# A decoder block's mixer with chunk matrices kept as 32x32 diagonal blocks, alternating small products, split attention scores and a solver tied to its place in VectorE's queue

## The chip, the cores and the metric

The kernel runs on one core of a Trainium2 chip. The metric is the time of one execution in device microseconds, from the first to the last instruction with what lies around them; lower is better. The five engines of the core are called PE (TensorE, matrix products), DVE (VectorE), ACT (ScalarE), POOL (GpSimd) and SP (SyncE, which issues most of the DMAs here). Each works through its own instructions in the order in which they are queued.

## The reference, cut to what matters

One decoder layer for 512 tokens of width 1024, in fp32. A projection of the normalized input feeds two mixers side by side, whose outputs are concatenated and projected back; an expert retrieval layer (PEER) and a gated embedding follow. The two mixers are what the change is about.

```python
def block(bi):                      # differential attention, 4 heads of 2 x 64, blocks of 128 queries
    s = jnp.einsum('bhcqd,bhckd->bhcqk', qb, k).astype(f32)
    causal = key_pos[None, :] <= (start + jnp.arange(Q_BLOCK))[:, None]
    pr = jax.nn.softmax(jnp.where(causal, s, -jnp.inf), axis=-1)
    a = pr[:, :, 0] - lam * pr[:, :, 1]
    return jnp.einsum('bhqk,bhkv->bhqv', a.astype(v.dtype), v)
...
def step(state, inp):               # RWKV-7, 8 heads of 64, one token after the other
    r_t, d_t, k_t, v_t, kk_t, a_t = inp
    sa = jnp.einsum('bhij,bhj->bhi', state, -kk_t)
    state = (state * d_t[:, :, None, :] + sa[..., None] * (kk_t * a_t)[:, :, None, :]
             + v_t[..., None] * k_t[:, :, None, :])
    return state, jnp.einsum('bhij,bhj->bhi', state, r_t)
```

## The kernel before

**Tiling.** The 512 tokens are four blocks b0 to b3 of 128, and a block is four chunks of 32 tokens for the RWKV mixer. Inside a chunk the recurrence is written as matrix products: for each head a matrix of products between the tokens is needed, of which only the pairs inside one chunk count. A block's matrix of a head has 128x128 entries, so the four 32x32 blocks on its diagonal are the ones that count; the rest is set to zero by a mask.

**Stages.** The mixer stage lies between about 125 and 440 us of the span; after it come the output projection, the expert layer and the tail, none of which the change touches, and each of which needs the whole of the mixer's output. The mixer has two phases.

- First phase, to about 277 us: `rw_prepare` runs for each block, woven with the projections of the attention's q, k and v (`acc` matmuls, whose operands are split into two fp32r parts, hi and lo). It makes four transposes (`ptr`), then the four masked matrices: `psA` products of beT and ktT with art, masked by DVE into `aab`, `arb`, `aak`, `ark` (L549 to L554), and two products of a masked matrix with v (`pg`, L569). `da_prepare` transposes q and k of the attention (`ptq`), and ACT copies them out.
- Second phase, from 277 us: per block `rw_solved` (`pwu`, `pmt`, `prp`), `rw_states` (four steps of `pst`), `rw_out` (`py`) and, per attention head, `da_block`: scores `psS` (L765, fp32, then L766, which adds the causal mask as a product with the identity), a row maximum on DVE (`sm`, L769), an exponential on ACT (L770), the weighted difference of two exponentials on DVE (`pexp`, L775), transposes (`pta`), the product with v (`po`). `ple_proj` (`accr` matmuls) is woven in.

**The solver.** `rw_solve(half)` inverts the chunk matrices of two blocks with 31 steps on DVE, each a product `sol_p` (L593) and a sum `sol_x` (L595). Half 0 runs in the first phase, half 1 in the second; its result goes to DRAM and comes back as `tt`, which `pwu` of block b2 needs first.

**What sets the order.** The code says in which order the pieces are emitted (generators that are woven), but a list scheduler then orders the instructions of each engine, which are executed in that order. `self.behind(x, y)` puts x after y in this order and nothing else. Tiles come from pools with a fixed number of buffers (tags `p2`, `p4`); a piece waits when its pool has none free.

## Time and profile before

| | us |
|---|---|
| median of 3 runs | 1839.75 (1837.05 to 1845.11) |
| the profiled execution | 1837.09 |
| its span, first to last instruction | 1835.4 |
| PE busy | 1728.9 (94% of the span) |
| DVE busy | 1425.6 (78%) |
| ACT busy | 746.7 (41%) |
| POOL busy | 604.7 (33%) |

The share of busy time is an average over all stages: PE's 94% comes mostly from the expert layer, after 600 us. A row of a group of instructions gives the line of the kernel, the engine, the operation, the tiles (output <- inputs), the shapes and the count; then the busy time, the mean of one in ns, and the idle time of the engine ahead of these instructions with what ended it. PE's matmuls overlap, so sums over them can exceed the time that passed; where that matters, starts are compared. An fp32 matmul is two PE instructions, an fp32r matmul one.

### The profile page before, as it was taken

What the parts mean: (1) busy time and instruction counts of PE and PEld (TensorE: products, weight loads), DVE (VectorE), ACT (ScalarE), POOL (GpSimd) and SP (SyncE); (2) the same over time, 40 slices, a digit from 0 to 9 for tenths busy, and PEclk for the clock granted to TensorE, in tenths of its full rate; (3) what the DMA queues carried; (4) which work ended last, traced back from release to release, by engine and by line L of the source; (5) the groups of instructions that cost most, each with busy time, mean ns of one, the idle gap of its engine ahead of it and who ended that gap; (6) DMA issues with size and microseconds to landing.
All of it is one profiled execution on the core that took longest, in us unless ns stands there. A gap on an engine that the chain in (4) does not pass through costs nothing.

```text
span 1835.4 us, 28662 instructions
## 1 busy us (share of the span) xinstructions
PE 1728.9 (94%) x10458; PEld 1468.2 (80%) x10458; DVE 1425.6 (78%) x3216; ACT 746.7 (41%) x1382; POOL 604.7 (33%) x425
## 2 busy tenths in 40 slices
PE   7889996998899888999999999999999999999998
PEld 6766764766777787998777888889899999999986
DVE  5366787675569998888888888887888888888885
ACT  5353332432345654444344333333333333333354
POOL 2650011111046663001111133234545555555530
PEclk9896996999999999999999999999999999999999
DMA  7451233433332343446666587778989898989891
GB/s 232 137 149 55 75 114 79 129 80 127 117 120 71 125 127 115 132 139 216 206 209 197 187 272 249 254 246 292 313 302 317 300 316 303 312 303 316 303 332 58
DMA packets 150417, 363.71 MB, mean 198 GB/s; under 512 B 43922, under 2 KB 58510, under 8 KB 150148
## 3 DMA queue, kind: packets, MB, share of 16 engines
q1 hardware_dynamic: 113412, 227.65, 38.7%
q0 software_dynamic: 36864, 134.23, 21.5%
q8 instruction: 82, 1.34, 0.3%
q14 instruction: 59, 0.48, 0.1%
HBM read 332.61 MB, written 21.36 MB: 193 GB/s over the span
## 4 chain that ended last, share of the span: by engine, by line
PE 67%; DVE 19%; issue 3%; ACT 3%; POOL 0%; DMA 0%; SPq 0%; DVEq 0%; ACTq 0%; POOLq 0%
PE po L1278 21%; PE phid L1142 8%; PE phid L1144 8%; PE phid L1143 8%; PE pg L1247 2%; DVE wlo L133 2%; PE psA L549 2%; DVE ids L1091 2%; ACT whi L129 1%; DVE rest L985 1%; PE psS L765 1%; DVE jj L1235 1%; PE accr L239 1%; PE accr L237 1%; PE accr L238 1%
## 5 line engine op out<-in xcount | busy, mean ns | idle before, releaser
L133 DVE TENSOR_TENSOR wlo<-wraw,whi 128x1024 fp32r<-128x1024 f32 x243 | 297.5, 1224 | 150.6 <-ACT whi L129 150.5
L129 ACT ACTIVATE whi<-wraw 128x1024 fp32r<-128x1024 f32 x276 | 291.4, 1057 | 171.3 <-PE phid L1143 59.0
L1144 PE MATMUL phid<-u2dhi,wlo 128*128 128x384 f32 x1024 | 347.3, 339 | 12.8 <-POOL wlo L133 12.8
L1142 PE MATMUL phid<-u2dhi,whi 128*128 128x384 f32 x1024 | 350.4, 342 | 1.0 <-ACT row L1151 1.0
L1143 PE MATMUL phid<-u2dlo,whi 128*128 128x384 f32 x1024 | 346.4, 338 | 0.0
L1301 POOL DMA_INDIRECT row<-in_peer_u_dram,idx x128 | 189.8, 1483 | 403.2 <-DVE row L1313 219.7
L1301 POOL DMA_INDIRECT row<-in_peer_v_dram,idx x128 | 186.1, 1454 | 277.0 <-DVE h L1317 194.7
L1278 PE MATMUL po<-whi,chi 128*128 128x512 f32 x768 | 243.9, 398 | 1.2 <-ACT row L1151 1.2
L1278 PE MATMUL po<-whi,clo 128*128 128x512 f32 x768 | 243.1, 398 | 1.7 <-DVE clo L135 0.4
L1278 PE MATMUL po<-wlo,chi 128*128 128x512 f32 x768 | 241.4, 395 | 0.0
L1144 PEld LDWEIGHTS phid<-u2dhi,wlo 128*128 128x128 f32 x1024 | 194.3, 190 | 14.8 <-POOL wlo L133 14.7
L1142 PEld LDWEIGHTS phid<-u2dhi,whi 128*128 128x128 f32 x1024 | 194.6, 190 | 5.8 <-ACT row L1151 1.3
L1143 PEld LDWEIGHTS phid<-u2dlo,whi 128*128 128x128 f32 x1024 | 194.1, 190 | 3.7
L1278 PEld LDWEIGHTS po<-whi,clo 128*128 128x128 f32 x768 | 143.0, 188 | 42.3 <-DVE clo L135 9.0
L1278 PEld LDWEIGHTS po<-wlo,chi 128*128 128x128 f32 x768 | 144.4, 188 | 34.2
L1317 DVE SCALAR_TENSOR_TENSOR h<-row,ids,h 128x1024 f32<-128x1024 f32 x128 | 164.0, 1281 | 1.6
L129 ACT ACTIVATE chi<-gelu 128x384 fp32r<-128x384 f32 x128 | 67.4, 526 | 240.1 <-DVE gelu L1255 121.8
L1278 PEld LDWEIGHTS po<-whi,chi 128*128 128x128 f32 x768 | 141.1, 188 | 25.6 <-ACT row L1151 1.5
L1313 DVE SCALAR_TENSOR_TENSOR row<-row,xn 128x1024 f32<-128x1024 f32 x128 | 153.7, 1220 | 0.0
L1151 ACT ACTIVATE gelu<-phid 128x384 f32<-128x384 f32 x86 | 42.3, 492 | 266.9 <-PE phid L1144 266.9
L133 POOL TENSOR_TENSOR wlo<-wraw,whi 128x1024 fp32r<-128x1024 f32 x33 | 78.4, 2386 | 126.4 <-ACT whi L129 114.7
L201 PE MATMUL acc<-whi,uhi 128*128 128x512 f32 (+1 forms) x224 | 89.6, 404 | 16.7 <-ACT whi L129 9.5
(439 smaller groups left out, 2884.7 us busy)
## 6 DMA issues: line engine op xcount, KB each, us to landing
wraw<-in_peer_uT_dram SPq DMA_DIRECT2D x128, 512.0 KB
wraw<-in_peer_v_dram SPq DMA_DIRECT2D x128, 512.0 KB
wraw<-in_w_in_dram SPq DMA_DIRECT2D x24, 512.0 KB
wraw<-in_peer_w_q_dram SPq DMA_DIRECT2D x16, 512.0 KB
ahead<-row SPq DMA_DIRECT2D x42, 192.0 KB
gelu<-ahead SPq DMA_DIRECT2D x42, 192.0 KB
wraw<-in_w_out_dram SPq DMA_DIRECT2D x8, 512.0 KB
zp<-z SPq DMA_DIRECT2D x12, 224.0 KB
```

Source lines behind the costliest of these rows:

```text
L129: self.last_hi = nc.scalar.activation(hi, src, AF.Copy, **({} if g is None else {"scale": g}))
L133: self.last_lo = eng.tensor_tensor(lo, src, hi.bitcast(F32), op=OP.subtract)
L201: nc.tensor.matmul(o, hi[:, k, s], whi, start=(k == 0), stop=False)
L549: nc.tensor.matmul(ps[:, mm, :, :], lhs[q, m * 128:(m + 1) * 128], art[q, m, :, :], start=True, stop=True)
L1142: nc.tensor.matmul(ps, whi[:, s], hi[:, k, :], start=(k == 0), stop=False)
L1143: nc.tensor.matmul(ps, whi[:, s], lo[:, k, :], start=False, stop=False)
L1144: nc.tensor.matmul(ps, wlo[:, s], hi[:, k, :], start=False, stop=(k == KC - 1))
L1151: nc.scalar.activation(g, ps, AF.Gelu)
L1278: nc.tensor.matmul(outs[b, e], lhs[:, s], rhs[:, 512 * e:512 * e + 512], start=(c == 0 and rhs is vhi and lhs is chi), stop=(c == NKEY - 1 ...
L1301: nc.gpsimd.indirect_dma_start(out=row, out_offset=None, in_=a["peer_u" if kind == "U" else "peer_v"], in_offset=bass.IndirectOffsetOnAxis ...
L1313: nc.vector.scalar_tensor_tensor(row, row, 1.0, xn0, op0=OP.mult, op1=OP.mult, accum_out=hid0[:, k:k + 1])
L1317: nc.vector.scalar_tensor_tensor(acc0, row, hid0[:, k:k + 1], acc0, op0=OP.mult, op1=OP.add)
```

## The change

It does five things, all in the mixer stage.

1. `diagonal()` replaces the masked 128-wide matrices. The products are made for the 32x32 blocks on the diagonal alone: 32 matmuls of 64 rows by 32 columns for each of beT and ktT, in an order (`corners()`) in which successive ones use other halves of PE's rows and other quarters of its columns. DVE masks each result with two operations (before: eight), and one tile `ab` (or `ak`) of 128x8x2x32 replaces two of 128x8x128. `mask2` is cut accordingly.
2. The products that used the wide matrices follow: `pg` becomes 32 matmuls of 32x32 weights for each output, the `wu` part of `py` 32 per block, and `prp` (8 of 128-row contraction) becomes 32 inside the `pmt` tile, so DVE adds four quarters (L660) in place of one whole.
3. `py` is made for both halves together, its products in the order of `corners()`.
4. The attention's q and k are split into fp32r parts by `da_prepare` (ACT makes hi, DVE lo), and a score is three fp32r matmuls (hi.hi, hi.lo, lo.hi) in place of one fp32 matmul; both score tiles of a head are started together, and the two causal products come after them.
5. Each step of the solver is put `behind` the DVE instruction last named `self.anchor`, which `rw_prepare`, `diagonal()` and `da_block` set as they are emitted. The pools become p2 32 (28) and p4 12 (14).

```diff
     def p2(self, name, shape=(128, 512), dt=F32):
-        return self.pages.tile(list(shape), dt, name=name, tag="p2", bufs=28)
+        return self.pages.tile(list(shape), dt, name=name, tag="p2", bufs=32)
 
     def p4(self, name, shape=(128, 1024), dt=F32):
-        return self.pages.tile(list(shape), dt, name=name, tag="p4", bufs=14)
+        return self.pages.tile(list(shape), dt, name=name, tag="p4", bufs=12)
...
-        for x, dram in ((aak, self.d_xg[b][:, 512:1024]), (ark, self.d_yk[b])):
-            pg = psum.tile([128, 8, 64], F32, name="pg", tag="mm")
-            for h in range(8):
-                nc.tensor.matmul(pg[:, h, :], x[:, h, :], v[:, h * 64:h * 64 + 64], start=True, stop=True)
+        for x, dram in ((0, self.d_xg[b][:, 512:1024]), (1, self.d_yk[b])):
+            pg = psum.tile([128, 8, 64], F32, name="pg", tag="mm")
+            for h in range(8):
+                for c in range(4):
+                    q = slice(32 * c, 32 * c + 32)
+                    nc.tensor.matmul(pg[q, h, :], ak[q, h, x, :], v[q, h * 64:h * 64 + 64], start=True, stop=True)
...
+    def corners(self):
+
+        return [(i % 2, (i // 2 + 2 * (i % 2)) % 4) for i in range(8)]
+
+    def diagonal(self, psum, lhs, art, name):
+
+        nc = self.nc
+        ps = [psum.tile([128, 4, 2, 32], F32, name="psA", tag="mm") for s in range(2)]
+        for m in range(4):
+            for s, c in self.corners():
+                q, d = slice(64 * s, 64 * s + 64), slice(32 * c, 32 * c + 32)
+                nc.tensor.matmul(ps[s][d, m, :, :], lhs[q, m * 128 + 32 * c:m * 128 + 32 * c + 32], art[q, m, :, d],
+                                 start=True, stop=True)
+        a = self.p2(name, [128, 8, 2, 32])
+        for s in range(2):
+            self.anchor = nc.vector.tensor_tensor(
+                a[:, s:8:2, :, :], ps[s], self.mask2[:, None, :, :].to_broadcast([128, 4, 2, 32]), op=OP.mult)
+        return a
...
-            nc.vector.tensor_tensor(pr[:, :n, :m], x[:, :n, :m], u[:, None, :m, t].to_broadcast([128, n, m]),
-                                    op=OP.mult)
+            self.behind(nc.vector.tensor_tensor(pr[:, :n, :m], x[:, :n, :m],
+                                                u[:, None, :m, t].to_broadcast([128, n, m]), op=OP.mult), self.anchor)
...
-            nc.scalar.activation(mt[:, c, :, :], pm, AF.Copy)
+            for h in range(8):
+                m, o = h // 2, slice(64 * (h % 2), 64 * (h % 2) + 64)
+                nc.tensor.matmul(pm[o, m, 64:96], wu[q, 0, h, :], st["ab"][q, h, 1, :], start=True, stop=True)
+            nc.scalar.activation(mt[:, c, :, :], pm[:, :, 0:64], AF.Copy)
+            nc.vector.tensor_tensor(st["rtT"][:, :, q], pm[:, :, 64:96], st["rtT"][:, :, q], op=OP.add)
         st["mt"] = mt
-        pr = psum.tile([128, 4, 128], F32, name="prp", tag="mm")
-        for h in range(8):
-            m, o = h // 2, 64 * (h % 2)
-            nc.tensor.matmul(pr[o:o + 64, m, :], wu[:, 0, h, :], st["arb"][:, h, :], start=True, stop=True)
-        nc.vector.tensor_tensor(st["rtT"], pr, st["rtT"], op=OP.add)
...
+            ps = [psum.tile([128, 512], F32, name="psS", tag="acc", bufs=4) for c in range(2)]
+            for i, j in ((0, 0), (0, 1), (1, 0)):
+                for c in range(2):
+                    o = slice(64 * c, 64 * c + 64)
+                    nc.tensor.matmul(ps[c][:, :nk], qT[i][o, h, :], kT[j][h // 2][o, h % 2, :nk],
+                                     start=i + j == 0, stop=i == 1)
             for c in range(2):
-                o = slice(64 * c, 64 * c + 64)
-                ps = psum.tile([128, 512], F32, name="psS", tag="acc", bufs=4)
-                nc.tensor.matmul(ps[:, :nk], qT[o, h, :], kT[h // 2][o, h % 2, :nk], start=True, stop=True)
-                nc.tensor.matmul(ps[:, b * 128:nk], self.ident_r, self.causal, start=False, stop=True,
+                nc.tensor.matmul(ps[c][:, b * 128:nk], self.ident_r, self.causal, start=False, stop=True,
                                  skip_group_check=True)
```

The next two pieces show DVE where the second phase begins: the first three score maxima (`sm`), then the solver's half 1. Before, the steps of the solver stand in one row up to the 24th, and the first `pexp` comes behind them; this is the start and the end of that run.

```order
L769 TENSOR_REDUCE sm<-psS 128x1 x3
L593 TENSOR_TENSOR sol_p<-sol_x,sol_u 128x2
L595 TENSOR_REDUCE sol_x<-sol_p 128x1
...
L593 TENSOR_TENSOR sol_p<-sol_x,sol_u 128x12x24
L773 RECIPROCAL smf<-sm 128x1
L595 TENSOR_REDUCE sol_x<-sol_p 128x12
L774 SCALAR_TENSOR_TENSOR smf<-smf,sm,nlam 128x1
L593 TENSOR_TENSOR sol_p<-sol_x,sol_u 128x12x25
L775 SCALAR_TENSOR_TENSOR pexp<-pexp,smf 128x128
L595 TENSOR_REDUCE sol_x<-sol_p 128x12
L651 TENSOR_TENSOR rtT<-prp,rtT 128x512
```

With the change four steps come first, then the chain of the first head (L787, L792 to L794 are the lines of L769, L773 to L775) and the new additions to rtT.

```order
L604 TENSOR_TENSOR sol_p<-sol_x,sol_u 128x2x5
L606 TENSOR_REDUCE sol_x<-sol_p 128x2
L787 TENSOR_REDUCE sm<-psS 128x1
L660 TENSOR_TENSOR rtT<-pmt,rtT 128x4x32 x2
L792 RECIPROCAL smf<-sm 128x1
L793 SCALAR_TENSOR_TENSOR smf<-smf,sm,nlam 128x1
L794 SCALAR_TENSOR_TENSOR pexp<-pexp,smf 128x128
L604 TENSOR_TENSOR sol_p<-sol_x,sol_u 128x3x6
L660 TENSOR_TENSOR rtT<-pmt,rtT 128x4x32
L606 TENSOR_REDUCE sol_x<-sol_p 128x3
L604 TENSOR_TENSOR sol_p<-sol_x,sol_u 128x3x7
```

So the first `pexp` moved from behind the 25th step's product to ahead of the fifth step, and the last steps moved back into the heads of the second block.

The following two pieces show PE in the first phase, at the chunk matrices of b0 (`ptl` and `plw` belong to b1's preparation).

```order
L549 MATMUL psA<-art,beT 128x256 x4
L466 MATMUL ptl<-ident,zsl 64x128
L549 MATMUL psA<-art,beT 128x256 x4
L467 MATMUL ptl<-ident,zsl 64x128
L549 MATMUL psA<-art,ktT 128x256 x4
L468 MATMUL ptl<-ident,zsl 128x128
L549 MATMUL psA<-art,ktT 128x256 x4
L569 MATMUL pg<-zs,aak 128x64 x8
L569 MATMUL pg<-zs,ark 128x64 x8
L475 MATMUL plw<-w_up,lw 128x512
```

```order
L578 MATMUL psA<-art,beT 32x64 x32
L471 MATMUL ptl<-ident,zsl 64x128
L472 MATMUL ptl<-ident,zsl 64x128
L473 MATMUL ptl<-ident,zsl 128x128
L578 MATMUL psA<-art,ktT 32x64 x32
L561 MATMUL pg<-zs,ak 32x64 x64
L480 MATMUL plw<-w_up,lw 128x512
```

The sixteen wide products became 64 small ones and the sixteen of `pg` 64, at the same place among PE's other work.

The last two pieces show PE at the products of the first block in the second phase, between two heads' scores.

```order
L643 MATMUL pmt<-bhr,wu 64x64 x4
L766 MATMUL psS<-causal_r,ident_r 128x128
L643 MATMUL pmt<-bhr,wu 64x64 x28
L650 MATMUL prp<-arb,wu 64x128 x8
```

```order
L654 MATMUL pmt<-bhr,wu 64x64 x3
L658 MATMUL pmt<-ab,wu 64x32 x8
L654 MATMUL pmt<-bhr,wu 64x64 [waits PE_49]
L654 MATMUL pmt<-bhr,wu 64x64 x7
L658 MATMUL pmt<-ab,wu 64x32 x8
L783 MATMUL psS<-causal_r,ident_r 128x128
L654 MATMUL pmt<-bhr,wu 64x64 [waits DVE_49]
L654 MATMUL pmt<-bhr,wu 64x64 x7
L658 MATMUL pmt<-ab,wu 64x32 x8
```

The products of `prp` moved into the four chunks of `pmt`, and the third chunk (and the fourth, behind this piece) now waits for DVE's semaphore, since DVE has to read the buffer of the first (and the second) before it is written again.

## Rows read from the trace of the kernel before

**Rows 1.** The page's head.

```profile
span 1835.4 us, 28662 instructions
```

**Rows 2.** Busy time by stretch; behind the engines granted clock, DMA share, GB/s.

```profile
225.00:250.00 25.00, 21.16 (x101) 15.24 (x101) 24.05 (x73) 11.62 (x22) 0.00 (x0) 0.86 0.19 64
...
275.00:300.00 25.00, 14.94 (x127) 11.17 (x126) 17.99 (x56) 7.36 (x16) 5.10 (x4) 0.76 0.59 122
300.00:325.00 25.00, 20.02 (x135) 14.27 (x136) 16.36 (x36) 4.66 (x19) 0.00 (x0) 0.63 0.10 27
...
350.00:375.00 25.00, 25.00 (x273) 17.66 (x272) 17.36 (x53) 8.36 (x20) 7.96 (x6) 1.00 0.46 130
...
277.00:440.00 163.00, 137.03 (x1455) 101.69 (x1454) 118.12 (x359) 53.54 (x136) 19.58 (x15) 0.89 0.34 82
```

**Rows 3.** Waits by engine and line, 277 to 325: total, times, longest.

```profile
ACT pexp L770 <- issue: 12.3, 1, 12.3
...
PE pta L778 <- DVE pexp L775: 7.9, 1, 7.9
```

**Rows 4.** DVE's groups of instructions, 277 to 440.

```profile
L593 DVE TENSOR_TENSOR sol_p<-sol_x,sol_u 128x2 f32<-128x2 f32 (+30 forms) x31 | 15.4, 498 | 1.9 <-POOL sol_u L589 1.0
...
L595 DVE TENSOR_REDUCE sol_x<-sol_p 128x1 f32<-128x2 f32 (+30 forms) x31 | 10.6, 342 | 0.9
```

**Rows 5.** DVE's groups, 125 to 277, each shape apart.

```profile
L135 DVE SCALAR_TENSOR_TENSOR wlo<-wraw,g_mix,whi 128x512 fp32r<-128x512 f32 x16 | 12.6, 799 | 6.3 <-ACT whi L129 6.3
L552 DVE TENSOR_TENSOR aak<-psA,mask 128x256 f32<-128x256 f32 x16 | 6.7, 421 | 6.2 <-PE psA L549 6.2
```

**Rows 6.** PE's groups, 125 to 277.

```profile
L549 PE MATMUL psA<-art,ktT 64*128 64x256 f32 x64 | 16.1, 460 | 0.0
L549 PE MATMUL psA<-art,beT 64*128 64x256 f32 x64 | 13.0, 433 | 1.7 <-DVE arb L554 1.7
L569 PE MATMUL pg<-zs,ark 128*128 128x64 f32 x64 | 9.4, 311 | 0.0
```

**Rows 7.** PE's timeline at the matrices of b0: start, duration, instructions.

```profile
142.70 2.08 PE L549 MATMUL psA<-art,beT 64*128 64x256 f32 x8
...
160.65 2.02 PE L475 MATMUL plw<-w_up,lw 65*128 65x512 f32 x2
```

**Rows 8.** PE's timeline in the second phase, two attention products and small ones.

```profile
326.65 0.70 PE L765 MATMUL psS<-kT,qT 64*128 64x256 f32 x2
327.27 0.33 PE L766 MATMUL psS<-causal_r,ident_r 128*128 128x128 f32 x1
...
328.84 0.39 PE L239 MATMUL accr<-whi,plo 128*128 128x512 f32 x1
329.07 0.40 PE L237 MATMUL accr<-whi,phi 128*128 128x512 f32 x1
...
329.87 1.14 PE L710 MATMUL py<-state,rtT 64*32 64x64 f32 x24
330.94 0.70 PE L765 MATMUL psS<-kT,qT 64*128 64x256 f32 x2
...
363.73 0.68 PE L667 MATMUL pst<-uv,bk 64*64 64x64 f32 x16
364.25 0.63 PE L675 MATMUL pst<-state,mt 64*64 64x64 f32 x16
```

**Rows 9.** PE's groups, 277 to 440.

```profile
L765 PE MATMUL psS<-kT,qT 64*128 64x128 f32 (+3 forms) x64 | 27.2, 509 | 5.2 <-ACT pexp L770 4.5 <-ACT pp L817 0.7
...
L766 PE MATMUL psS<-causal_r,ident_r 128*128 128x128 f32 x32 | 10.9, 340 | 0.0
...
L702 PE MATMUL py<-wu,arb 128*128 128x64 f32 x64 | 8.4, 274 | 0.0
...
L650 PE MATMUL prp<-arb,wu 128*64 128x128 f32 x64 | 5.2, 315 | 0.7 <-ACT mt L645 0.7
```

**Rows 10.** PE's timeline where block b2 begins.

```profile
377.79 1.95 PE L631 MATMUL pwu<-xg,tt 128*128 128x128 f32 x16
```

More of the change, by code (lines that the diff above doesn't have):

```diff
@@ L269, in mixer_consts @@
         same_chunk(self.tri_gt, 2)
-        self.mask2 = pool.tile([128, 2, 128], F32, name="mask2")
-        nc.gpsimd.memset(self.mask2, 1.0)
-        same_chunk(self.mask2[:, 0, :], 1)
-        same_chunk(self.mask2[:, 1, :], 0)
+        full = self.p2("mask", [128, 2, 128])
+        nc.gpsimd.memset(full, 1.0)
+        same_chunk(full[:, 0, :], 1)
+        same_chunk(full[:, 1, :], 0)
+        self.mask2 = pool.tile([128, 2, 32], F32, name="mask2")
+        for c in range(4):
+            q = slice(32 * c, 32 * c + 32)
+            nc.gpsimd.tensor_copy(self.mask2[q], full[q, :, q])
         self.chunk_ind = pool.tile([128, 4], F32, name="chunk_ind")
@@ L506, in rw_prepare @@
         nc.vector.tensor_mul(rt, r, e_in)
[L507 removed]
+        self.anchor = nc.vector.tensor_mul(aa, aa, kk)
         yield
@@ L536, in rw_prepare @@
                 if src is rt:
[L537 removed]
+                    self.anchor = nc.vector.tensor_copy(st["rtT"], pt)
         yield
[L540 to L557 removed]
@@ new lines, in rw_prepare @@
+        st["ab"] = self.diagonal(psum, bet, art, "ab")
+        yield
+        for c in range(4):
+            ad = self.ad[b // 2]
+            dst = bass.AP(tensor=ad.tensor, offset=ad.offset + (b % 2 * 32 + c * 8) * 1024,
+                          ap=[[32, 32], [1024, 8], [1, 32]])
+            nc.sync.dma_start(dst, st["ab"][32 * c:32 * c + 32, :, 0, :])
+        ak = self.diagonal(psum, ktt, art, "ak")
+        yield
+        for x, dram in ((0, self.d_xg[b][:, 512:1024]), (1, self.d_yk[b])):
+            pg = psum.tile([128, 8, 64], F32, name="pg", tag="mm")
+            for h in range(8):
@@ L697, in rw_out @@
         yk = st["yk"].rearrange("p (h v) -> p h v", h=8)
-        for par in range(2):
-            py = psum.tile([128, 4, 64], F32, name="py", tag="mm")
-            o = slice(64 * par, 64 * par + 64)
-            for m in range(4):
-                nc.tensor.matmul(py[:, m, :], st["arb"][:, 2 * m + par, :], st["wu"][:, 1, 2 * m + par, :],
-                                 start=(m == 0), stop=False, skip_group_check=True)
-            for c in range(4):
+        py = [psum.tile([128, 4, 64], F32, name="py", tag="mm") for par in range(2)]
+        for m in range(4):
+            for par, c in self.corners():
+                q = slice(32 * c, 32 * c + 32)
+                nc.tensor.matmul(py[par][q, m, :], st["ab"][q, 2 * m + par, 1, :], st["wu"][q, 1, 2 * m + par, :],
+                                 start=(m == 0), stop=st["s"][c] is None and m == 3, skip_group_check=True)
+        for m in range(4):
+            for par, c in self.corners():
                 s = st["s"][c]
@@ L707, in rw_out @@
                     continue
-                q = slice(32 * c, 32 * c + 32)
-                for m in range(4):
-                    nc.tensor.matmul(py[q, m, :], st["rp"][o, m, q], s[o, m, :], start=False,
-                                     stop=(m == 3), skip_group_check=True)
-            nc.vector.tensor_tensor(y[:, par:8:2, :], py, yk[:, par:8:2, :], op=OP.add)
+                o, q = slice(64 * par, 64 * par + 64), slice(32 * c, 32 * c + 32)
+                nc.tensor.matmul(py[par][q, m, :], st["rp"][o, m, q], s[o, m, :], start=False,
+                                 stop=(m == 3), skip_group_check=True)
+        for par in range(2):
+            nc.vector.tensor_tensor(y[:, par:8:2, :], py[par], yk[:, par:8:2, :], op=OP.add)
         mean = sm.tile([128, 8], F32, name="mean")
@@ L874, in mixers @@
             self.lambdas(cpool)
-            zd, qT, kT, vs = {}, {}, [p4(f"kT{i}", [128, 2, T]) for i in range(2)], {}
+            zd, qT, kT, vs = {}, {}, [[p4(f"kT{x}{i}", [128, 2, T], F32R) for i in range(2)]
+                                  for x in ("hi", "lo")], {}
             def eat_z(b, ps):
```

54 lines of the change are left out of this document (17 added, 37 removed).

## The prediction

> **What bounds the kernel now.** I read the busy time by stretch first, since only the mixer stage is touched. Its second phase, 277 to 440 us, has PE busy for 137.0 of 163 us and DVE for 118.1 [rows 2]. The stages behind it need its whole output, so I let a microsecond gained or lost here move the end by a microsecond. Inside the phase two regimes alternate. At 350 to 375 PE is busy all 25.0 us at full clock, DVE 17.4: PE's own work sets the pace there. At 275 to 325 PE is busy for 14.9 + 20.0 of 50 us, and its granted clock is only 0.76 and 0.63 [rows 2]: it idles, and the idling is followed by work at the lower clock level (1.2 GHz in place of 2.4). The waits of this stretch say why: PE's `pta` waits once for 7.9 us for DVE's `pexp`, and ACT's exponential stands for 12.3 us without a releaser that the profile shows [rows 3]. In this stretch DVE works off the solver's 62 instructions, 15.4 + 10.6 = 26.0 us [rows 4], in one row; every row maximum and `pexp` of a head stands behind them in DVE's queue (the order of the front part shows it).
>
> In the first phase PE and DVE pass work to each other: at 225 to 250 DVE is busy for 24.05 of 25 us and PE drops to 21.2 at clock 0.86 [rows 2]; a mask waits for its `psA` (6.2 us in sum [rows 5]), the next `psA` for a mask (1.7 us [rows 6]).
>
> **The change, first phase.** *Masks.* A block has 16 mask operations of 0.42 us [rows 5]. It will have four, of as many elements each: twelve fewer, 5.0 us a block, 20.2 us in all. *New DVE work.* The lo parts of q are four operations of 128x512, at most the 0.80 us of the lo part shown, and those of k eight of 128x256 at 0.42 [rows 5]: 3.2 + 3.4 = 6.6 us, mostly where DVE is full (b2). ACT makes as many copies as before.
>
> *Small products.* `psA` takes 16.1 + 13.0 us and `pg` twice 9.4 [rows 6]: 47.9. The new form is 32 matmuls for each of two operands and 32 for each of two `pg`, two instructions each: 256 instructions a block, 1024 in all. No row shows a product of this size in this order, so I bound one by its neighbours. The 64x64 products of `pst`, which alternate the two halves of PE's rows, start 16 instructions in 0.52 us (363.73 to 364.25), 33 ns each; the `py` products, which stay in one half, start 24 in 1.07 us, 45 ns each [rows 8]. I take 33, as `corners()` alternates too: 34 us at full clock. Block b0 runs mostly at the lower clock level: from 142.70 to 160.65 it takes 17.95 us [rows 7], and 256 instructions at 66 ns are 17: a gain of 1. The other three blocks have about 47.9 less 17.95, 30.0, and come to 768 x 33 ns = 25.3: 5. With 1.7 us of mask waits gone and the masks' 5.0 us shorter chain showing where DVE is the later one (b2: 5.0 less 3.4 of new work, 1.6), and half a microsecond in each of the others, 1.5, the sum is 10.8 and I take **-11** for the phase. The bounds: at 45 ns a product the 1024 cost 46 us, 2 under today, with the waits -3; at most all 20.2 us of masks leave the path, -20.
>
> **The change, second phase.** *Scores.* The fp32 score of 256 columns takes 0.62 us (326.65 to 327.27), an fp32r product of 512 columns 0.23 (328.84 to 329.07) [rows 8]. Over four heads, two halves and 128 to 512 columns there are 10,240 columns: 40 x 0.62 = 24.8 us before, 3 x 20 x 0.23 = 13.8 after: **-11**. The causal products (10.9 us [rows 9]) stay. If the two score tiles of a head, which use different halves of PE's rows, overlap, 13.8 becomes 6.9 and the term -18. It lies on the path where PE is full (350 to 375); where DVE is the later one it is hidden, and the bound is 0.
>
> *rp and py.* The rp products become 256 instructions: at 33 ns 8.4 us against 5.2. The `wu` part of `py` also becomes 256: 8.4 against 8.4 [rows 9]. The 240 state products of `py`, alternating now, go from 45 to 33 ns: -2.9. Together **0** (at 45 ns for all, +9). DVE's sixteen quarter additions cost at most 0.42 each [rows 5] in place of four whole ones: at most 4 us more, in a phase where DVE is idle for 45 of 163.
>
> *The solver.* Of the 50 us at 275 to 325 PE idles 15.0; and by the clock rows 14.9 x 0.24 + 20.0 x 0.37 = 11 us of its busy time are the price of the lower level [rows 2]: 26 us. The steps are not cheaper, they only stand between the heads: the first `pexp` now follows the four shortest steps where it followed 24. What is late next is block b2, whose `pwu` needs the solver's result, but it starts only at 377.79 [rows 10], and the last step stands among the heads of the second block. I take half of the loss, **-13**: the first heads' chain of maximum, exponential and `pexp` remains, and so does the wait of PE at the seam of the phases. The bounds are 0 and -26.
>
> *New wait.* `pmt` of the third and fourth chunk waits for DVE's addition, with the rest of PE's queue behind it. A wait can be one or two solver steps, 0.5 + 0.34 us each in the mean [rows 4]; eight places, most of them with DVE idle: **+1**, at most 8 x 0.84 = +7. A page pool of 12 large buffers in place of 14 holds two more tiles of k and four fewer `arb`, so as many are free.
>
> Check: 118.1 us of DVE work plus at most 4 in 163 - 23 = 140 us is 87%: room, but not for 26 + 18 more. Sum: -11 - 11 + 0 - 13 + 1 = -34. The profiled execution took 1837.1 us (span 1835.4 [rows 1]), 2.7 under the median, so 1803 by its own time and **1805** by the median.
>
> **A rule against it.** The four quarters of `pg` and of `py` that work on different rows of PE write one PSUM tile. The two row halves of `pst` write one tile too, and start 33 ns apart on average [rows 8], so I let them overlap. The Trainium skill (TensorEngine Tiling (Array Packing), Gotcha 1: PSUM Pressure) says that different row tiles cannot access the same PSUM bank at once. By that rule these products would come one after the other; the `pst` row speaks against it, but no row shows quarters. It is the third rival.
>
> **The rivals.**
>
> 1. *The solver's time only moves.* DVE has 118 us of work in the phase; if `pexp`, maxima and states are late by the steps between them, each head waits a little and the loss of 26 us is met again, and the faster scores are half hidden. For it: DVE's queue is in order, and 26 us of steps must fit between heads. Against it: PE is full at 350 to 375 with DVE at 17.4. Then -11 - 5 = -16, **1823**. Chance 0.20.
> 2. *More overlap.* Score halves overlap (-7 more), the small products come under 33 ns (1536 by 5 ns, -8), and 5 us more of the solver's loss return: -54, **1786**. For it: nothing but other quarters of PE's columns in `corners()`. Chance 0.14.
> 3. *`pg` and `py` in single file.* If their 768 instructions do not overlap, each costs the 65 ns of a `pst` pair: 768 x 32 ns = +24.6 on the sum, -9.5, **1830**. Against it: the `pst` row. Chance 0.09.
> 4. *Slower: PE cannot start small products fast enough.* All 1536 (1024, and 512 of rp and `py`) replace 47.9 + 5.2 + 8.4 = 61.5 us. If no two overlap, they cost 65 ns each, 100 us: +38, less 11 for scores and 13 for the solver, +14, **1854**. It decides from (61.5 + 24) / 1536 = 56 ns a product; the nearest rows show 33 and 45. Chance 0.07.
>
> **The numbers.** The forecast has 0.50. Faster by over 0.5% (9.2 us, about what a measurement of this kernel can tell: its three runs spread by 0.4%) are forecast and rivals 1 and 2: 0.84; within it rival 3: 0.09; slower rival 4: 0.07. The range, 1780 to 1830, leaves out rival 4, the upper half of rival 3 and the far end of rival 2. The forecast's own range is 1792 to 1815, from all 26 us of the solver's loss to 3 of them.
>
> **What would show it.** Mask operations: 16 of about 0.42 us in all. `psA` and `pg` of b3: some 8.4 us from first to last start. `psS` starts: 0.7 us for a head's six products at 256 columns. No `pta` wait of over 3 us and PEclk over 0.8 at the start of the second phase; `pwu` of b2 without a wait for `tt`. The phases end at about 266 and 406. The prediction is wrong if small products start over 45 ns apart, if `pwu` of b2 waits for the solver, or if DVE is busy over nine tenths of the second phase with PE waiting for it.

## The result, and the profile after

The changed kernel takes 1824.1 us (median of 4 runs, 1822.0 to 1826.1) against 1839.7 for the kernel before: ratio 0.9911, 95% interval 0.9886 to 0.9937. It is faster by 15.6 us where 34.7 were forecast. The profiled execution took 1825.1 us, its span 1823.4.

I split both traces at two events: the first score `psS`, where the second phase begins, and the start of the last `ocat` of `rw_out`, with which it ends. These are the busy times of the two phases (columns as in [rows 2]), first of the kernel before:

```profile
100.00:277.05 177.05, 161.81 (x735) 119.15 (x733) 126.67 (x335) 74.70 (x121) 28.47 (x26) 0.88 0.33 95
277.05:439.33 162.28, 136.98 (x1455) 101.69 (x1454) 117.45 (x358) 53.49 (x136) 19.58 (x15) 0.89 0.34 82
```

and of the changed kernel:

```profile
100.00:251.49 151.49, 128.71 (x1508) 95.44 (x1506) 118.69 (x299) 74.60 (x122) 31.46 (x27) 0.94 0.37 102
251.49:422.70 171.21, 146.11 (x1870) 112.82 (x1870) 114.09 (x369) 55.35 (x137) 20.84 (x15) 0.76 0.34 87
```

The first phase is 25.6 us shorter (forecast 11), the second 8.9 us *longer* (forecast 23 shorter). The rest, from the last `ocat` to the end of the span, went from 1396.1 to 1400.7, a part that the prediction left as it was. The three make 12.1 us, the difference of the two profiled executions; the medians differ by 15.6. In both profiles of the changed kernel PE works at half the clock from 478 to 485 us, behind the mixer; no run isolates why.

Read the second phase so: PE's busy time times the mean granted clock is about its work at full clock. It fell from 137.0 x 0.89 = 122 us to 146.1 x 0.76 = 111, by 11 us, as the terms for scores, rp and `py` together had said (-11 and 0). The time in which PE does nothing stayed: 25.3 and 25.1 us. What grew is the price of the lower clock level, busy time less work: from 15 to 35 us. That is where the gain went.

In the 25-us rows that answer to [rows 2] the same is seen piecewise:

```profile
150.00:175.00 25.00, 21.02 (x225) 15.07 (x213) 19.33 (x60) 15.63 (x26) 0.00 (x0) 0.93 0.28 83
...
250.00:275.00 25.00, 19.35 (x186) 15.34 (x175) 4.89 (x25) 8.19 (x20) 2.50 (x2) 0.56 0.73 171
...
300.00:325.00 25.00, 21.46 (x179) 16.88 (x179) 21.22 (x69) 7.19 (x19) 0.00 (x0) 0.57 0.42 102
...
350.00:375.00 25.00, 22.45 (x194) 16.81 (x192) 15.09 (x44) 8.75 (x22) 3.04 (x4) 0.68 0.35 77
```

At 250 to 275 DVE is busy for 4.9 of 25 us. DVE's timeline there says why (start, duration, instruction, idle time ahead with its releaser):

```profile
260.95 0.17 DVE L606 TENSOR_REDUCE sol_x<-sol_p 128x2 f32<-128x10 f32 x1
270.45 0.29 DVE L787 TENSOR_REDUCE sm<-psS 128x1 f32<-128x128 f32 x1 [9.33 <-PE psS L783]
270.66 0.48 DVE L660 TENSOR_TENSOR rtT<-pmt,rtT 128x128 f32<-128x128 f32 x2
...
271.62 0.35 DVE L794 SCALAR_TENSOR_TENSOR pexp<-pexp,smf 128x128 f32<-128x128 f32 x1
```

After four solver steps DVE stands 9.3 us before a row maximum. PE's queue has `pwu` and `pmt` ahead of that score's causal product; PE waits 2.3 and 0.8 us for their loads and works `pwu` off at the lower level, in 3.75 us:

```profile
261.38 3.75 PE L642 MATMUL pwu<-xg,tt 128*128 128x128 f32 x16 [2.30 <-DMA xg<-d_xg]
265.97 0.69 PE L654 MATMUL pmt<-bhr,wu 32*64 32x64 f32 x8 [0.84 <-DMA bhr<-d_bh]
...
269.94 0.47 PE L783 MATMUL psS<-causal_r,ident_r 128*128 128x128 f32 x1
```

Before, `pwu` took as long (3.78 us) but waited for no load. The first `pexp` comes 20.1 us after the first score; before it came about 21. The 27 steps left then stand among the heads, up to 331.6 us (DVE busy 21.2 of 25 us at 300 to 325).

The small products, at full clock in b3 of the first phase:

```profile
243.75 0.86 PE L578 MATMUL psA<-art,beT 64*32 64x64 f32 x64
244.54 0.50 PE L203 MATMUL acc<-whi,ulo 128*128 128x512 f32 x1
...
248.31 1.88 PE L561 MATMUL pg<-zs,ak 32*32 32x64 f32 x120
250.12 0.50 PE L203 MATMUL acc<-whi,ulo 128*128 128x512 f32 x1
```

64 instructions of `psA` in 0.79 us are 12 ns each, 120 of `pg` in 1.81 us 15 ns; I had taken 33. In the second phase the products with 32 rows are the dear ones (groups as in [rows 9]):

```profile
L654 PE MATMUL pmt<-bhr,wu 32*64 32x64 f32 x256 | 15.1, 268 | 3.6 <-DVE rtT L660 2.0 <-DMA bhr<-d_bh 0.8 <-ACT wu L643 0.6
L780 PE MATMUL psS<-kThi,qThi 64*128 64x128 f32 (+3 forms) x32 | 13.2, 480 | 5.7 <-ACT pexp L788 2.6 <-ACT pp L836 2.2 <-ACT dav L903 0.9
L658 PE MATMUL pmt<-ab,wu 32*64 32x32 f32 x256 | 12.9, 249 | 0.0
L780 PE MATMUL psS<-kTlo,qThi 64*128 64x128 f32 (+3 forms) x32 | 10.5, 387 | 0.0
L780 PE MATMUL psS<-kThi,qTlo 64*128 64x128 f32 (+3 forms) x32 | 10.3, 386 | 0.0
L712 PE MATMUL py<-wu,ab 32*32 32x64 f32 x256 | 6.4, 235 | 0.0
```

The rp products take 12.9 us of busy time, where `prp` took 5.2, and the scores 34.0, where they took 27.2. These are sums over products that overlap, many of them at the lower level, so they do not show the work; run e6 does.

### The profile page after: what moved, and what is told of

The parts are those of the page before. It is cut to its first block, busy times and chain, and to the rows that moved or that the text cites. A ratio compares the mean times of both kernels' runs of the same rounds, so it can differ in the third digit from the quotient of the medians.

```text
span 1823.4 us, 30976 instructions
## 1 busy us (share of the span) xinstructions
PE 1706.2 (94%) x11642; PEld 1454.9 (80%) x11642; DVE 1414.5 (78%) x3192; ACT 747.6 (41%) x1382; POOL 608.6 (33%) x429
## 4 chain that ended last, share of the span: by engine, by line
PE 56%; DVE 10%; ACT 2%; issue 1%; POOL 1%; DVEq 0%; POOLq 0%; ACTq 0%
PE po L1298 22%; PE phid L1162 10%; PE phid L1164 10%; PE phid L1163 10%; PE pg L1267 2%; DVE wlo L133 2%; ACT whi L129 1%; DVE jj L1255 1%; POOL wlo L133 1%; PE accr L1452 1%; PE accr L1453 1%; PE accr L1451 1%; DVE gelu L1275 1%; DVE gi L1258 1%; DVE ids L1111 1%
## 5 line engine op out<-in xcount | busy, mean ns | idle before, releaser
L1164 PE MATMUL phid<-u2dhi,wlo 128*128 128x384 f32 x1024 | 347.7, 340 | 12.1 <-POOL wlo L133 12.1
L1298 PEld LDWEIGHTS po<-whi,chi 128*128 128x128 f32 x768 | 141.1, 188 | 25.6 <-ACT row L1171 1.5
```

Source lines behind the costliest of these rows:

```text
L1164: nc.tensor.matmul(ps, wlo[:, s], hi[:, k, :], start=False, stop=(k == KC - 1))
L1298: nc.tensor.matmul(outs[b, e], lhs[:, s], rhs[:, 512 * e:512 * e + 512], start=(c == 0 and rhs is vhi and lhs is chi), stop=(c == NKEY - 1 ...
```

## The experiments

Theory C: the second phase's PE work fell, and the clock took the gain back. Rival W: VectorE's place in the queue is what costs, PE's work does not matter. Times are medians; each ratio is to runs of the kernel before on the same chip. One execution of the kernel before varies (1826 to 1851, its median on five chips 1835.0 to 1846.6), the changed one less (1822.0 to 1826.1 in five). A version has 4 to 10 executions, so differences of 4 us between two versions are not clear of scatter. The phases and clocks are those of one profiled execution each, which in e4, e12, e14 and e18 was the slowest of its version, 4 to 8 us over the median.

| run | us | ratio to before (95%) | first, second phase | PE busy x clock, second |
|---|---|---|---|---|
| before / again (e15) | 1839.7 / 1834.3 | | 177.1, 162.3 / 170.4, 163.8 | 137.0 x 0.89 / 139.0 x 0.87 |
| changed / again (e16) | 1824.1 / 1825.2 | 0.9911 (0.9886 to 0.9937) | 151.5, 171.2 / 150.0, 172.1 | 146.1 x 0.76 / 146.2 x 0.77 |
| e1 solver's place undone | 1820.0 | 0.9883 (0.9823 to 0.9943) | 147.6, 166.3 | 140.7 x 0.79 |
| e2 fp32 scores | 1811.6 | 0.9836 (0.9776 to 0.9897) | 150.9, 162.6 | 144.2 x 0.78 |
| e3 pmt in pairs of chunks | 1822.8 | 0.9891 (0.9855 to 0.9926) | 151.0, 169.6 | 141.8 x 0.76 |
| e4 rp behind pmt | 1824.2 | 0.9888 (0.9826 to 0.9949) | 151.5, 173.9 | 150.2 x 0.74 |
| e5 e2 + solver free | 1821.7 | 0.9914 (0.9878 to 0.9950) | 150.0, 174.9 | 148.6 x 0.75 |
| e6 e2, scores not paired | 1818.2 | 0.9892 (0.9859 to 0.9925) | 149.9, 166.7 | 147.5 x 0.81 |
| e7 useless work at waits | 1832.0 | 0.9961 (0.9925 to 0.9997) | 153.9, 176.5 | 159.1 x 0.80 |
| e8 no alternation | 1825.0 | 0.9928 (0.9896 to 0.9961) | 150.9, 171.9 | 146.6 x 0.76 |
| e9 e2, beT wide, full rp | 1813.5 | 0.9857 (0.9810 to 0.9904) | 160.0, 150.3 | 131.1 x 0.86 |
| e10 e2 + useless work in pmt | 1831.5 | 0.9974 (0.9943 to 1.0005) | 150.5, 176.7 | 161.6 x 0.78 |
| e11 before, scores paired | 1846.4 | 1.0020 (0.9991 to 1.0050) | 170.4, 175.0 | 146.2 x 0.79 |
| e12 before, solver's place | 1840.8 | 0.9997 (0.9963 to 1.0031) | 182.0, 169.0 | 149.5 x 0.84 |
| e13 e2, full-row rp | 1808.4 | 0.9846 (0.9814 to 0.9877) | 155.0, 155.9 | 133.3 x 0.84 |
| e14 changed, full-row rp | 1817.3 | 0.9891 (0.9862 to 0.9921) | 149.0, 169.3 | 137.6 x 0.80 |
| e17 e13, tail of y on POOL | 1813.8 | 0.9892 (0.9856 to 0.9927) | 151.2, 160.2 | 129.3 x 0.85 |
| e18 e13 + solver free | 1814.2 | 0.9885 (0.9856 to 0.9915) | 153.8, 167.0 | 138.3 x 0.81 |

**e1, the solver's place undone.**

```diff
-            self.behind(nc.vector.tensor_tensor(pr[:, :n, :m], ...), self.anchor)
+            nc.vector.tensor_tensor(pr[:, :n, :m], ...)
```

> The changed kernel with its fifth part undone: the solver's steps are free in VectorE's order, all else stays. Changed kernel 1824, kernel before 1840. Theory C (the second phase does less PE work, but at the lower clock level for 78 of its 171 us, and the clock is lost in PE's short waits and in the row-quarter products of pmt and rp): the solver's run of about 26 us stands ahead of the first heads again, PE waits for pexp as before, 5 to 13 us slower, 1829 to 1837. Rival W (VectorE's place in the queue is what costs: in the changed kernel VectorE stands idle for most of 250 to 270 us behind a row maximum, and does the solver later, when the heads need it): 5 to 15 us faster, 1809 to 1819.

1820.0, 4 us under the changed kernel, with times that overlap (1816 to 1825 against 1822 to 1826): theory C's forecast of a slower kernel fell, and W's range was missed by 1 us. The steps ran at 254 to 284 us, in the gap in which DVE had stood idle and behind it.

**e2, fp32 scores.** One fp32 matmul for each tile, both tiles of a head still together.

```diff
-            for i, j in ((0, 0), (0, 1), (1, 0)):
-                for c in range(2):
-                    ... matmul(ps[c][:, :nk], qT[i][o, h, :], kT[j][h // 2][o, h % 2, :nk], ...)
+            for c in range(2):
+                ... matmul(ps[c][:, :nk], qT[o, h, :], kT[h // 2][o, h % 2, :nk], start=True, stop=True)
```

> The changed kernel with its fourth part undone: scores are one fp32 matmul again, and the eighteen or so microseconds of lo and hi copies for q and k go back to plain copies. Theory C (PE's work sets the second phase): the 11 us at full clock that the split saves come back, nearly half of them at the lower level, less some 3 us of VectorE work that is saved ahead of the phase: 1833 to 1842. Rival W (PE is not what the phase waits for): 1819 to 1826, no slower.

12.5 us *faster* than the changed kernel, against both theories; all of its times (1809.3 to 1817.5) lie under all of the changed kernel's, while the intervals of the ratios just overlap. PE's timeline of e2 shows why fp32 scores cost so little:

```profile
375.32 1.13 PE L777 MATMUL psS<-kT,qT 64*128 64x512 f32 x4
376.38 0.44 PE L779 MATMUL psS<-causal_r,ident_r 128*128 128x128 f32 x2
```

Both fp32 scores of 512 columns start and end within 1.06 us. That is as long as one alone takes in the kernel before,

```profile
387.12 1.12 PE L765 MATMUL psS<-kT,qT 64*128 64x512 f32 x2
388.17 0.33 PE L766 MATMUL psS<-causal_r,ident_r 128*128 128x128 f32 x1
```

so on different halves of PE's rows they overlap. The scheduler left the two next to each other in 8 of the 16 heads. Five of a head's six split products take 0.89 us where it alternated the halves,

```profile
387.06 0.50 PE L780 MATMUL psS<-kThi,qThi 64*128 64x512 f32 x1
387.06 0.72 PE L780 MATMUL psS<-kTlo,qThi 64*128 64x512 f32 x2
387.40 0.62 PE L780 MATMUL psS<-kThi,qTlo 64*128 64x512 f32 x2
387.95 0.44 PE L783 MATMUL psS<-causal_r,ident_r 128*128 128x128 f32 x2
```

(the sixth, the first of its tile, lies earlier), and the three of one tile 0.90, 1.80 a head, where it did not:

```profile
352.61 0.50 PE L780 MATMUL psS<-kThi,qThi 64*128 64x512 f32 x1
352.95 0.40 PE L780 MATMUL psS<-kTlo,qThi 64*128 64x512 f32 x1
353.19 0.39 PE L780 MATMUL psS<-kThi,qTlo 64*128 64x512 f32 x1
353.51 0.33 PE L783 MATMUL psS<-causal_r,ident_r 128*128 128x128 f32 x1
```

A whole head at 384 columns takes 0.72 us split and alternated (348.96 to 349.68), 0.85 as an fp32 pair (320.61 to 321.46 in e2). So the split saves little that pairing alone would not: PE's work in the phase is 111.0 us with it and 112.5 without, and its lo parts are 6.1 us of work for DVE in the first phase.

**e3, e4, other orders of pmt and rp.** In e3 two chunks alternate; in e4 the rp products stand behind pmt in tiles of their own.

```diff
-        for c in range(4):
+        for c2 in (0, 2):
+            pm = [psum.tile([128, 4, 96], F32, name="pmt", tag="mm") for j in range(2)]
...
+                    for par, j in ((0, 0), (1, 1), (0, 1), (1, 0)):
```

> The changed kernel, but the pmt and rp products of two chunks alternate, in two PSUM tiles, so that successive products use two quarters of PE's rows and both halves of its columns; before, all products of a chunk stood in one quarter of the rows. The results are the same. Theory C: pmt and rp together take less than the 27 ns a product that they now take (512 instructions, 28 us of busy time at mixed clock), and the clock does not fall in them: three low stretches of 6.8, 13.5 and 3.8 us shrink; 8 to 18 us faster, 1806 to 1816. Rival W: the products are not on the path, 0 to 4 us faster, 1820 to 1824.

> The changed kernel, but the rp products stand behind the four chunks of pmt in PSUM tiles of their own, two chunks alternating, so that no chunk of pmt waits for VectorE's addition. The results are the same. If the new wait of pmt for VectorE is what costs (rival A): all of its 2.0 us of PE idle time and the fall of the clock behind it come back, 5 to 12 us faster, 1812 to 1819. Theory C, in which the single-quarter products drop the clock themselves: the half of them that alternates now helps, 3 to 8 us. Rival W: nothing, 1822 to 1826.

1822.8 and 1824.2: no change that can be told, as rival W had said of both. In e3 the two groups fell from 28.0 to 17.0 us of busy time, PE's waits for `rtT` rose from 2.0 to 3.8 us, and the clock stayed at 0.76. PE's work was 3 us less (107.8), and the time the same.

**e5, both undone.** The edits of e1 and e2.

> The changed kernel with its fourth and fifth part undone: one fp32 score per tile (the two score tiles of a head still started together), solver steps free in VectorE's order. Theory, that the two parts cost independently (the first runs gave 12 us for the scores, 4 for the solver's place): 1803 to 1812, the fastest so far. Rival, that both only shift the same waits: 1810 to 1818, no faster than the one with fp32 scores alone.

1821.7: the rival's side, and worse. By the medians the solver's place is worth 10 us with fp32 scores and costs 4, within scatter, with split ones; the parts do not add.

**e6, fp32 scores, each with its causal product behind it.**

> The changed kernel with fp32 scores and with each score tile followed by its own causal product again, as in the kernel before. Theory P: what makes fp32 scores fast in the changed kernel is that the two of a head stand next to each other on different halves of PE's rows and overlap (both of 384 columns in 0.85 us start to start, where the kernel before took about that for each); without it 10 to 12 us of PE work at full clock come back, 1818 to 1828. Rival S: it is the split itself that is dear (three products, lo parts on VectorE), and the pairing counts for nothing: 1809 to 1815.

1818.2: pairing is worth 6.6 us, the lower end of theory P. Here the work of PE shows in the time: without the pairing it is 7 us more in the second phase (147.5 x 0.81 = 119.5 against 112.5), and the phase 4.2 us longer.

```profile
249.89:416.62 166.73, 147.47 (x1838) 105.91 (x1838) 114.44 (x369) 55.22 (x137) 22.98 (x20) 0.81 0.37 88
```

This run is also the changed kernel with its fourth part undone whole, so it prices the prediction's term for the scores. With split and paired scores the second phase has 8 us less PE work (111.0), and the changed kernel is 5.9 us *slower* (1824.1; 1822.0 to 1826.1 against 1816.9 to 1820.2, though the intervals of the ratios overlap; a gain of 11 us lies outside them): PE's idle time in the phase is 25.1 us in place of 19.3, the price of the lower level 35 in place of 28.

**e7, useless dense work at PE's waits.**

```diff
+            for _ in range(0 if q else 24):
+                nc.tensor.matmul(ps[:, 3], self.ident_r, self.causal, start=True, stop=True)
...
+            for _ in range(8 if b < 3 else 0):
+                nc.tensor.matmul(pt[:, 3, :], self.ident_r, self.causal, start=True, stop=True)
```

> The changed kernel with useless dense work for PE: eight 128x128 products of the identity with the causal mask ahead of each pta of the first three token blocks, into a part of its PSUM tile that is not read, and 24 ahead of each pwu, which overwrites them; about 11 us of PE time at full clock if all of it shows. The results are the same. Theory C (the second phase is slow since PE's clock is low for 78 of its 171 us, and that is since PE has too little to do in short stretches): the mean clock of the second phase rises from 0.76 to 0.83 or more, and the time falls by 2 to 15 us, 1809 to 1822. Rival (the low clock hurts little; PE's waits are for VectorE and ACT): the extra work shows, 3 to 12 us slower, 1827 to 1836.

The clock rose to 0.80, not the 0.83 that was forecast, and PE's idle time fell to 17.4 us, but the run is 7.9 us slower: theory C's remedy fell. Some 16 us of added work (159.1 x 0.80 against 111; 11 were meant) cost 5.3 us of the phase.

**e8, no alternation** in `corners()`.

```diff
-        return [(i % 2, (i // 2 + 2 * (i % 2)) % 4) for i in range(8)]
+        return [(i // 4, i % 4) for i in range(8)]
```

> The changed kernel with the order of its small products (psA, both parts of py) no longer alternating: first the four quarters of one half, then the four of the other. Theory O (the first phase gained 25.6 us and not 11 since small products overlap far better than the 33 ns taken: psA starts 12 ns apart): in this order two neighbours share a half of PE's rows, psA goes to 25 to 45 ns, 512 of them, and the state products of py to 45: 6 to 20 us slower, 1830 to 1844. Rival: the masks alone made the first phase faster, and the order of the products is worth 0 to 4 us, 1822 to 1828.

1825.0: the alternation is worth nothing here. `psA` still starts every 12 ns (64 in 0.79 us from 196.99), so products on other quarters of PE's columns overlap as well.

**e9, matrices of beT wide, full-row rp**, on e2; the pools are 28 and 14 again.

> The changed kernel with fp32 scores (1811.6 us), and with the matrices of beT made wide and masked whole again, so that rp is eight products of full 128-row weights behind pmt, and no chunk of pmt waits for VectorE; ktT, pg and py stay in 32x32 blocks. Theory Q (the rp products in one quarter of PE's rows double the stretch of such products, and the clock falls behind it: 13.5 us low at block b2 in the run with fp32 scores, none there in the kernel before, with the same pwu and pmt ahead): no low stretch behind pmt of b2 and b3, the second phase 8 to 15 us shorter than its 162.6, the first 3 to 8 us longer for the masks: 1800 to 1812. Rival: the second phase stays at 160 to 166 us and the masks show: 1814 to 1822.

The second phase fell by 12.3 us, the first grew by 9.1: 1813.5, between the two forecasts. PE's work in the second phase stayed (131.1 x 0.86 = 112.8); the price of the lower level fell from 32 to 18 us. The low stretch behind `pmt` of b2 did not go, as theory Q wanted: it lies at 352 to 365 here. Two things changed in the second phase (rp and pmt's wait), and the first phase came along, so e13 and e14 followed.

**e10, useless work between pmt and rp**, on e2.

> The changed kernel with fp32 scores (1811.6 us), and six useless 128x128 products of full rows between the pmt and the rp products of each chunk, into a part of the PSUM tile that is not read; 96 in all, some 7 us of PE time at full clock. The results are the same. Theory Q by way of activity (a long stretch of quarter-row products is what lets the clock fall): the low stretches behind pmt of b2 (13.5 us) and b3 (10.2) go, which gives back up to 11 us for 7: 1806 to 1814. Rival: they stay, and the extra work shows: 1816 to 1823.

20 us slower, and the low stretch behind `pmt` of b2 stayed: more activity there does not keep it away. PE's work rose by 13.6 us (161.6 x 0.78 against 112.5; 7 were meant), and the phase by 14.1, all of it.

**e11, e12, one part alone on the kernel before.**

> The kernel before (about 1840 us) with one thing changed: the two fp32 score products of a head stand next to each other, and the two causal products behind them. Theory P (pairing is what the fourth part is good for, not the split): at full clock up to 12 us of PE work go, of which the undoing in the changed kernel showed 6.6: 1829 to 1836. Rival: as long as the solver's run holds up the first heads, PE's work is not what the second phase waits for: 1837 to 1843.

> The kernel before with the fifth part alone: each solver step behind the VectorE instruction that the changed kernel names. The prediction's term: half of the 26 us that PE loses at 275 to 325 comes back, 1824 to 1830. Theory M (the solver's time only moves: in the changed kernel VectorE stood idle at the seam and did the steps later, and undoing the part made it 4 us faster with split scores but 10 us slower with fp32 ones): 1835 to 1845.

Neither helps: 1846.4 and 1840.8. e11 has 6 us less PE work in the second phase (146.2 x 0.79 = 115.5 against 121.9), and by its interval the kernel is at most 0.1% faster for it, 2 us; in the profiles its second phase is 12.7 us longer, in an execution 3 us over the median against one 3 us under. e12 is the prediction's solver term by itself: no change, and by its interval at most 7 us of the 13.

**e13, e14, full-row rp alone,** on e2 and on the changed kernel; POOL puts the wide weights together.

```diff
+        arb = self.p4("arb", [128, 8, 128])
+        nc.gpsimd.memset(arb, 0.0)
+        for c in range(4):
+            q = slice(32 * c, 32 * c + 32)
+            nc.gpsimd.tensor_copy(arb[q, :, q], st["ab"][q, :, 1, :])
...
+            nc.tensor.matmul(pr[o:o + 64, m, :], wu[:, 0, h, :], arb[:, h, :], start=True, stop=True)
```

> The changed kernel with fp32 scores (1811.6 us), and rp made by eight products of full 128-row weights behind the four chunks of pmt; the wide weights are put together by POOL from the 32x32 blocks just ahead of use (a memset and four copies a block). The first phase stays as in the changed kernel. Theory Q (the quarter-row rp products and the wait of pmt for VectorE cost the second phase 12 us): the first phase stays at 150 to 152 us, the second goes from 162.6 to 148 to 154; 1797 to 1805 and the fastest version. Rival (what the run with wide matrices gained in the second phase was only a shift from its longer first phase): 1809 to 1815.

> The changed kernel (1824 us) with the same edit as the run before it and nothing else: split scores and the solver's place stay. Theory Q: 171.2 us of second phase become 157 to 165, 1810 to 1818. Rival: 1821 to 1827.

1808.4 (3 us under e2, within scatter, and outside both forecasts) and 1817.3 (7 under the changed kernel, as theory Q said, though the second phase of its profile, 169.3, is not the 157 to 165 that Q asked for). Quarter-row rp costs up to 7 us, not 12. e13's upper end, 0.9877, lies under the changed kernel's lower one, 0.9886: it beats both kernels.

**e15, e16, second profiles.**

> The kernel before, unchanged, for a second profile: how far its phases vary from one execution to the next. The first profile had 177.1 us from 100 to the first score and 162.3 from there to the last ocat, with 36 us at the lower clock level in the second. If scatter is small: within 3 us of both. If the spread of its runs (1826 to 1851) sits in the mixer: one of the two phases is 5 us or more off, with as many low stretches more or fewer.

> The changed kernel, unchanged, for a second profile. The first had 151.5 us from 100 to the first score and 171.2 to the last ocat, 85 us at the lower level. Its four times lie within 4 us, so both phases should come within 3 us.

The changed kernel repeats within 1.5 us in each phase. Before, the first phase took 170.4, 6.7 less. The difference is in b0; these are its rows of the first and the second profile:

```profile
150.00:175.00 25.00, 23.18 (x73) 16.37 (x72) 14.39 (x40) 9.95 (x16) 0.00 (x0) 0.57 0.10 35
150.00:175.00 25.00, 21.36 (x112) 15.78 (x111) 18.58 (x62) 14.92 (x25) 0.00 (x0) 0.93 0.16 53
```

In the first PE is at the lower level from 148.0 to 168.5 us, in the second from 163.0 to 166.5 only. Two more versions have the first phase of the kernel before, e12 but for the solver's place: e11 is like the second profile there (0.93, first phase 170.4), e12 like the first (0.50, 182.0). So the first phase gained 19 to 27 us, and the second lost 7 to 10.

**e17, e18, VectorE's load and the solver's place, on e13.**

> The version with fp32 scores and full-row rp (e13, 1808.4 us), and the last three VectorE operations of rw_out (128x512, 0.69 us each) go to POOL for blocks b0 to b2: 6.2 us less VectorE work in the second phase, PE's the same. The results are the same. Theory V (short waits of PE for VectorE set the second phase, by themselves and by the low clock behind them): fewer waits of PE for pexp and rtT, the second phase 2 to 8 us shorter than 155.9, 1799 to 1806. Rival (VectorE's load does not matter, only what the order happens to be): 1806 to 1812.

> The version with fp32 scores and full-row rp (e13, 1808.4 us) without the solver's place: steps free in VectorE's order. The same undoing made the version with fp32 and quarter-row rp 10 us slower (1811.6 to 1821.7), the changed kernel 4 us faster. Theory V: what counts is whether pexp of the first heads is late; with the free order the steps stand in one run ahead of it, 4 to 12 us slower, 1812 to 1820. Rival: 1803 to 1811, the sign of the effect is chance.

e17 decides nothing: POOL was late with the wide weights, PE waited 11.4 us for them. e18 is 6 us slower than e13 by the medians, in theory V's range (the intervals of the ratios overlap), and PE's waits for `pexp` rose from 3.1 to 7.8 us.

**What the low clock follows.** In e13 at block b2 PE waits twice, 1.7 us in sum,

```profile
345.16 0.55 PE L798 MATMUL pta<-ident,pexp 128*128 128x128 f32 x3 [1.10 <-DVE pexp L795]
346.29 0.94 PE L811 MATMUL po<-dav,ah 128*128 128x128 f32 x6 [0.58 <-ACT ah L802]
```

and the clock falls at 351.7 and comes back at 365.3; in the kernel before that `pta` waits for nothing, and there is no fall:

```profile
375.83 0.55 PE L778 MATMUL pta<-ident,pexp 128*128 128x128 f32 x3
377.02 0.94 PE L791 MATMUL po<-dav,ah 128*128 128x128 f32 x6 [0.58 <-ACT ah L782]
```

The changed kernel shows it most plainly behind 2.55 us of waiting for ACT (rows of one us, PE busy first):

```profile
333.00:334.00 1.00, 0.00 (x0) 0.00 (x0) 0.84 (x2) 0.59 (x3) 1.00 (x1) 1.00 0.49 87
334.00:335.00 1.00, 0.87 (x4) 0.62 (x4) 0.29 (x2) 0.64 (x3) 0.03 (x1) 0.99 1.02 175
335.00:336.00 1.00, 1.00 (x4) 0.86 (x4) 0.82 (x3) 0.00 (x0) 0.00 (x0) 0.50 0.01 1
```

It then stays low to 342. Not every wait is followed by a fall, and I have no run in which the waits alone were taken away.

## Why the prediction was wrong

The direction and the first rival's time were right, the range held; the sum was wrong in both phases. The range held by luck: a first phase that gained more than its term made up for a second that lost time. None of the three signs that were to show the prediction wrong came: the small products start 12 to 18 ns apart, `pwu` of b2 waits for nothing, and DVE is busy for 114 of 171 us. The sign that did fail is the clock of over 0.8 at the start of the second phase: it is 0.56.

- **Masks and small products (-11): mis-sized, -19 to -27.** The mask operations came out as forecast: 16 of 0.42 us. The 33 ns a product, from `pst`, was the wrong row: 12 to 15 ns. e9, where the matrices of beT go back to wide (and the pools with them), gives 9.1 us of it. The lower level through most of b0 (0.57 at 150 to 175 before, 0.93 after) is no sure gain of the change: the second profile of the kernel before has 0.93 too, and most of the difference between -19 and -27 hangs on it. `corners()` is not the reason (e8).
- **The rule against it.** `pg`, whose four row quarters write one tile, starts every 15 ns, and the `wu` part of `py` every 18 (32 in 0.58 us from 408.54), near the 12 of `psA`, whose row halves write a tile each. The Trainium skill (TensorEngine Tiling (Array Packing), Gotcha 1: PSUM Pressure) says that different row tiles cannot use the same bank at once. In this order, each quarter with its own output partitions, the trace shows them overlapping (single file was priced at 65 ns), and rival 3 is out. Rival 2 had the overlap right, of the small products and of scores on different halves; its 1786 did not follow, since the second phase did not get shorter.
- **Scores (-11): the work fell as computed, the time did not.** This is the step that failed: "it lies on the path where PE is full". The term by itself is e6 against the changed kernel: 8 us less PE work, 5.9 us more time, so the bound 0 was too kind. PE's idle time and the price of the lower level took the work's place, 6 and 7 us. The reading of 350 to 375 went wrong in taking a PE that is busy for 25.0 of 25 us for the only limit there. My account is that PE with less work meets DVE and ACT earlier, waits in pieces of about a microsecond, and does what follows at the lower level; it fits the rows, but it is argued, not shown. How work turns into time here has no one rate: e11 (6 us less work, no faster), e3 (3 less, no faster) and e7 (16 more, 5.3 longer) speak for little, e6 against e2 (7 more, 4.2 longer) and e10 (13.6 more, 14.1 longer) for more than half or all. Nor was the split needed: paired fp32 scores (e2) leave 112 us of work.
- **The solver (-13): nothing that can be told.** This term failed too. Rival 1 had it: the time only moves. The first `pexp` is as late as before, since the wait for a score takes the place of the steps; e12 gives 0.9997 (0.9963 to 1.0031). One row maximum of the first heads stood inside the run of steps before, not all behind it: its score was not ready before 288.5 us, behind `pwu` and `pmt` in PE's queue, so not all of the lateness was the solver's. In other orders the same part is worth +4 (e1, within scatter), -10 (e5) and -6 us (e18).
- **rp and py (0): up to +7**, by e14. The size was right: products of one row quarter, in a row, start 30 ns apart at full clock (64 of `pmt` and rp from 397.54 to 399.46), near the 33 taken, and the state products of `py` 18 ns (32 from 386.48 to 387.06), better than that. What rp in quarter rows costs beyond its work no run splits up; the wait behind it is 2.0 us in sum, near the +1 taken (e4: no change).
- **Rival 1's 1823** is met by other terms than its own, which is luck as well: 8 to 16 more from the first phase, and the second phase not shortened but lengthened.

The cause of the longer second phase stays open: what orders its waits, and why the clock follows some of them. Its time ran from 150 to 177 us over these runs, at 108 to 127 us of PE work, 15 to 32 of PE's idle time, 15 to 39 for the lower level, and 110 to 120 of DVE's work; the solver's part seems to change its sign with the order of the rest.

## What to carry to other kernels

Price an engine's saved work by the wait that ends last once it is saved: here 8 us of it came back as 6 us of idle time, 7 at the lower clock level and a slower kernel. Count lower-level time as a term of its own (busy less busy times clock) before and after. Profile a kernel twice before explaining a difference of some microseconds in one stretch. Try the cheap half of a change first: starting two fp32 products on different row halves together cut PE's work nearly as far as the split did (112.5 and 111.0 us).

## What the runs showed of the hardware

- Small fp32 products on different 32-column quarters or row quarters start 12 to 18 ns apart (`psA` 64 in 0.79 us, `pg` 120 in 1.81, `py` 32 in 0.58); for `psA` the order of the halves makes no difference (e8).
- Two fp32 products of 64 rows on different halves of PE's rows take 1.06 us together at 512 columns (e2); one alone takes 1.05 (before).
- The same instructions of the first phase took 177.1 and 170.4 us in two executions; PE was at the lower clock level for 20.5 us of b0 in the first and for 3.5 in the second.
